# The post-norm of an output tile: gate first into on-chip memory, factor last in the operation that adds the stream

## The chip, the cores and the metric

The kernel runs on one core of one Trainium2 chip. The metric is the device time of one execution in microseconds (us). The core has a matrix engine (TensorE, PE in the profile; its weight loads are PEld), VectorE (DVE), ScalarE (ACT), GpSimd (POOL) and SyncE (SP), which issues the DMAs. Matrix products land in PSUM; everything else that is on the chip lies in SBUF.

## The reference

Four trunk layers work on 512 latent tokens and 256 context tokens of width 1024. Layer i uses the mixer i mod 3: latent attention with low-rank queries and keys (A, layers 0 and 3), banded window attention (B, layer 1), a gated long convolution by Fourier transforms (C, layer 2). Around every mixer stands the same frame. Cut to what matters here:

```python
def rmsnorm(x, g):
    return x * lax.rsqrt(jnp.mean(x * x, axis=-1, keepdims=True) + NORM_EPS) * g
...
h = rmsnorm(x, g_pre) * (1 + scale) + shift      # scale, shift, gate from the condition
y = mixer(h, ...)                                # ends in ... @ w_out
x = x + gate * rmsnorm(y, g_post)
```

Latent and context tokens have gates of their own. The last layer's output is the latent stream alone.

## The kernel before

The 768 tokens are six tiles of 128 (four latent, two context; the last layer handles four). A layer's mixer leaves its result, transposed, in one large block `og` of on-chip memory. Then `w_out_phase` goes over the tiles in a given order; below, tile 0 to 5 means the place in that order. For each tile it does the following.

- It splits the tile of `og` into a high and a low part (L613, L614) and multiplies both with the output weights: 48 matmuls of 128x512 (L622) into one of two PSUM tiles, `pb_70` and `pb_69`, which take turns. Each is 128x1024 in float32.
- `post` makes the new stream of the tile. ScalarE squares the product and sums along the row (L564); GpSimd makes the factor of the norm of the sum (`rstd`, L358 and L359: a scale and shift, and a power of minus one half); DVE multiplies the product by factor and gate, in place in PSUM (L566); DVE adds the stream to it (L567); SyncE stores the stream (L568).
- `pre` of the next layer follows at once, on the same tile: Square of the stream (L534), `rstd` on GpSimd, DVE's scaling into a slot `xs` (L537), eight transposes of 128x128 on PE (L543), scale and shift of the eight results back into `xs`, half of them on ScalarE (L548) and half on DVE (L550), and the split of `xs` into high and low part (L555 on ScalarE, L556 on DVE). After L556 `xs` is free.

Next the following layer's projections use the same two PSUM tiles: L577 to L579 where the channels stand on the partitions (keys and the like of layers 1 and 3), L588 behind layer 1. L442 are small matmuls that make the later layers' shifts, scales and gates. L230 (ScalarE) and L233 (GpSimd, in places DVE) split weights that a DMA has brought.

Slots of on-chip memory come from an arena of 13,760 float32 words per partition. `fs(D)` asks for one part of 1,024 words. While `og` is held, it takes 6,144 words, and seven parts are left for the streams of the tiles (`xt`), for `xs`, and for weights on their way. Of the first free ones, at most six (`turns_f`), the part freed longest ago is given out. Where the part has had another user, the new writer waits for the old reader.

The code is written tile by tile, but the order on each engine is not the order of the code: the framework's scheduler simulates the program on a timeline with its own costs and places every instruction on its engine. It also makes the semaphores. So an edit in `post` can move instructions of other lines.

Of the kernel before, what the change touches and what calls it, by code (L numbers as in the profile page):

```python
# [16 lines left out]
ALU = mybir.AluOpType  # L17
# [3 lines left out]
D = 1024  # L21
# [249 lines left out]
class Kern:  # L271
# [287 lines left out]
    def post(self, L, t, ys, xt, g):  # L559

        nc = self.nc
        s = 0 if t < 4 else 1
        ssq = self.col()
        nc.scalar.activation(self.trash, ys, AF.Square, accum_out=ssq)  # L564
        self.rstd(ssq, D)
        nc.vector.scalar_tensor_tensor(ys, ys, ssq, g[s].ap, op0=ALU.mult, op1=ALU.mult)  # L566
        nc.vector.tensor_tensor(xt.ap, xt.ap, ys, op=ALU.add)  # L567
        nc.sync.dma_start(out=self.xd[L + 1][t], in_=xt.ap)  # L568


# [1254 lines left out]
```

## Time and profile before

| quantity | value |
|---|---|
| time, median of three runs | 1950.36 us |
| the three runs | 1950.36, 1953.75 and 1942.91 us |
| the profiled execution's own time | 1947.24 us |
| its span in the profile | 1945.5 us |
| its mean granted TensorE clock | 0.989 of full speed |
| L566 / L567, mean of one | 1.29 / 1.22 us, 22 times each |
| L564, the Square | 1.00 us and 0.19 for its sum |

The span is what the profile shows between the first and the last instruction; the execution's own time contains a little around it. A row of the timeline gives the start, the duration, the engine, the line, the operation, what it writes and reads, and how many neighbours were put together; in brackets stands how long the engine was idle before it and what ended that. `pa` and `pb` are PSUM tiles, `arena_f`, `arena_r`, `swing_F` and `swing_R` parts of SBUF, `small` the column of sums and factors.

### The profile page before, as it was taken

How to read it: one execution, taken by the hardware profiler on the slowest of the kernel's cores; microseconds unless marked ns; L12 is line 12 of the kernel's file. 1: busy time of each engine (PE TensorE's matmuls, PEld its weight loads, DVE VectorE, ACT ScalarE, POOL GpSimd, SP SyncE). 2: the span in 40 equal slices, each digit the busy share in tenths (PEclk: the TensorE clock that was granted, in tenths of full speed). 3: DMA queues.
4: the chain of work that ended last, by engine and by line, in shares of the span. 5: the costliest groups of instructions: out<-in, count | busy, mean ns of one | idle time of the engine just before them, and what ended most of it. 6: DMA issues, size and time to landing. Idle time of an engine off the chain costs nothing. (4 is left out here: it accounts for less than half of the span.)

```text
span 1945.5 us, 30306 instructions
## 1 busy us (share of the span) xinstructions
PE 1815.3 (93%) x11628; PEld 1572.0 (81%) x11628; DVE 1176.2 (60%) x2364; ACT 812.6 (42%) x1687; POOL 517.7 (27%) x523
## 2 busy tenths in 40 slices
PE   5879799999999899999989999999998999999998
PEld 3657588999988888888868789999987777889986
DVE  6794234777755277777774356655567553477663
ACT  3473222545544255665654422222222353354451
POOL 5551000000213321222231444444445121000120
PEclk9999899999999999999999999999999999999999
DMA  7967420011133122222362622222222335310121
GB/s 218 270 185 232 140 75 25 23 33 34 55 108 109 55 65 66 77 77 66 119 204 100 200 82 77 75 74 71 75 65 68 115 121 153 86 34 23 44 76 54
DMA packets 186356, 186.31 MB, mean 96 GB/s; under 512 B 16600, under 2 KB 164952, under 8 KB 186212
## 3 DMA queue, kind: packets, MB, share of 16 engines
q1 hardware_dynamic: 186212, 184.39, 30.8%
q8 instruction: 91, 1.49, 0.3%
q14 instruction: 53, 0.43, 0.1%
HBM read 160.24 MB, written 24.12 MB: 95 GB/s over the span
## 5 line engine op out<-in xcount | busy, mean ns | idle before, releaser
L588 PE MATMUL pb<-arena_r 128*128 128x512 f32 (+1 forms) x1488 | 280.5, 342 | 2.1 <-DVE arena_f L1519 1.1
L341 ACT ACTIVATE arena_r<-pa 128x384 fp32r<-128x384 f32 (+2 forms) x382 | 175.2, 478 | 200.2 <-PE pa L898 67.2
L588 PEld LDWEIGHTS pb<-arena_r 128*128 128x128 f32 x1488 | 229.3, 189 | 33.1 <-ACT arena_r L1451 1.5
L342 DVE TENSOR_TENSOR arena_r<-pa,arena_r 128x384 fp32r<-128x384 f32 (+2 forms) x382 | 199.8, 537 | 79.4 <-ACT arena_r L341 77.4
L588 PE MATMUL pa<-arena_r,swing_R 128*128 128x512 f32 (+1 forms) x816 | 165.9, 355 | 0.6 <-DVE arena_r L342 0.4
L588 PEld LDWEIGHTS pa<-arena_r,swing_R 128*128 128x128 f32 x816 | 132.2, 188 | 21.8 <-DVE arena_r L342 0.6
L873 PE MATMUL pb<-arena_r 128*128 128x384 f32 (+1 forms) x720 | 141.4, 336 | 3.0 <-ACT arena_r L341 1.8
L233 POOL TENSOR_TENSOR swing_R<-arena_f,swing_R 128x1024 fp32r<-128x1024 f32 (+1 forms) x33 | 76.6, 2325 | 204.0 <-ACT swing_R L230 154.1
L873 PEld LDWEIGHTS pb<-arena_r 128*128 128x128 f32 x720 | 119.0, 188 | 5.1 <-ACT arena_r L341 2.5
L668 POOL TENSOR_TENSOR arena_f<-arena_f 128x128 f32<-128x128 f32 (+1 forms) x44 | 20.8, 474 | 364.0 <-DVE small L881 180.2
L622 PE MATMUL pb<-arena_r 128*128 128x512 f32 x480 | 115.2, 393 | 0.0
L358 POOL TENSOR_SCALAR small<-small 128x1 f32<-128x1 f32 x68 | 18.1, 266 | 350.8 <-ACT trash L704 136.0
L622 PEld LDWEIGHTS pb<-arena_r 128*128 128x128 f32 x480 | 89.5, 188 | 20.0 <-issue 1.1
L233 POOL TENSOR_TENSOR arena_r<-swing_F,arena_r 128x1024 fp32r<-128x1024 f32 x34 | 82.8, 2437 | 79.8 <-ACT arena_r L230 73.6
L912 PE MATMUL pa<-arena_r 128*128 128x256 f32 x624 | 91.4, 286 | 2.1 <-DVE arena_r L342 2.1
L912 PEld LDWEIGHTS pa<-arena_r 128*128 128x128 f32 x624 | 81.7, 189 | 4.8 <-ACT arena_r L341 2.5
L1068 PE MATMUL pa<-swing_R,arena_r 128*128 128x256 f32 x576 | 80.3, 289 | 5.1 <-DVE arena_f L348 3.8
L877 DVE TENSOR_REDUCE small<-pb 128x1 f32<-128x768 f32 (+1 forms) x80 | 67.5, 846 | 21.6 <-PE pb L873 20.8
L880 ACT ACTIVATE arena_f<-pb,small 128x768 f32<-128x768 f32 (+1 forms) x80 | 65.2, 816 | 33.6 <-DVE small L878 27.2
L1068 PEld LDWEIGHTS pa<-swing_R,arena_r 128*128 128x128 f32 x576 | 72.9, 192 | 7.3 <-DVE arena_f L348 5.2
L1049 PE MATMUL pa<-arena_r,swing_R 128*128 128x512 f32 (+1 forms) x384 | 74.2, 342 | 2.7 <-DVE arena_r L1075 1.1
L442 PE MATMUL pa<-arena_f,cst 128*32 128x256 f32 x744 | 55.7, 398 | 20.2 <-DMA arena_f<-in_w_mod_dram 20.1
(267 smaller groups left out, 4209.8 us busy)
## 6 DMA issues: line engine op xcount, KB each, us to landing
arena_f<-in_w_mod_dram SPq DMA_DIRECT2D x93, 512.0 KB, 4.8
swing_F<-in_c_w_in_dram SPq DMA_DIRECT2D x31, 512.0 KB, 4.9
kd<-arena_f SPq DMA_DIRECT2D x48, 256.0 KB, 3.7
arena_f<-in_a_w_in_dram SPq DMA_DIRECT2D x24, 512.0 KB, 3.7
arena_f<-kd SPq DMA_DIRECT2D x16, 768.0 KB, 5.2
arena_f<-in_b_w_in_dram SPq DMA_DIRECT2D x20, 512.0 KB, 3.7
x<-arena_f SPq DMA_DIRECT2D x18, 512.0 KB, 4.1
arena_f<-in_a_w_out_dram SPq DMA_DIRECT2D x16, 512.0 KB
```

The source lines that it names most:

```text
L233: eng.tensor_tensor(lo, view, hi.bitcast(F32), op=ALU.subtract)
L341: self.nc.scalar.activation(hi, src, AF.Copy)
L342: self.nc.vector.tensor_tensor(lo, src, hi.bitcast(F32), op=ALU.subtract)
L442: nc.tensor.matmul(ps[32 * j:32 * j + 32, n0:n0 + 256], self.cst[:, 4 * kh + j, :], w[:, j, :], start=(kh == 0), stop=(kh == 1), skip_grou ...
L588: nc.tensor.matmul(out, l, rhs(part, k, i), start=(k == 0 and q == 0), stop=(k == kt - 1 and q == 2))
L622: nc.tensor.matmul(ys[:, 512 * hf:512 * hf + 512], ov[:, part, k], wt[:, 0, 512 * hf:512 * hf + 512], start=(k == 0 and q == 0), stop=(k = ...
L873: nc.tensor.matmul(S[:, 512 * b:512 * b + w], l, r[:, k0 + w * b:k0 + w * b + w], start=(q == 0), stop=(q == 4))
L877: nc.vector.tensor_reduce(mx, Sv, axis=AX.XY, op=ALU.max)
L880: nc.scalar.activation(pr.v(nb, w), Sv, AF.Exp, bias=mx, scale=sc, accum_out=sm)
L912: nc.tensor.matmul(o[:, 0:256], vv[:, a_, kt % 3, P * hh:P * hh + P], ptv[i // nh][:, b_, i % nh], start=(i == 0 and q == 0), stop=(i == n ...
L1049: nc.tensor.matmul(o, l[:, k], self.h_at(h, part, k, t0, n), start=(k == 0 and i == 0), stop=(k == KD - 1 and i == 2))
L1068: nc.tensor.matmul(ps[:, 0:256], self.h_at(h, part, k, P * t, P), w, start=(k == 0 and i == 0), stop=(k == KD - 1 and i == 2))
```

## The change

`post` multiplies the product by the gate alone and puts the result into a slot `yg` of on-chip memory. This operation no longer reads the factor. The factor comes in the second operation, which multiplies `yg` by it and adds the stream, with both inputs in SBUF. The PSUM tile is read by the Square and by the first product, and written no more.

```diff
         s = 0 if t < 4 else 1
+        yg = self.fs(D)
         ssq = self.col()
         nc.scalar.activation(self.trash, ys, AF.Square, accum_out=ssq)
         self.rstd(ssq, D)
-        nc.vector.scalar_tensor_tensor(ys, ys, ssq, g[s].ap, op0=ALU.mult, op1=ALU.mult)
-        nc.vector.tensor_tensor(xt.ap, xt.ap, ys, op=ALU.add)
+        nc.vector.tensor_tensor(yg.ap, ys, g[s].ap, op=ALU.mult)
+        nc.vector.scalar_tensor_tensor(xt.ap, yg.ap, ssq, xt.ap, op0=ALU.mult, op1=ALU.add)
+        yg.free()
         nc.sync.dma_start(out=self.xd[L + 1][t], in_=xt.ap)
```

Two lines more stand above the rest, so every later line has a number that is two higher in the program after: the product is L567, the scale-and-add L568, the store L570, the Square L565, the matmul of the tile L624 (L622 before), the key projection L579 to L581 (L577 to L579), the projection behind layer 1 L590 (L588). `pre` keeps its numbers.

The scheduler places much anew. The following pieces show the engines at three transitions from one layer to the next.

First, DVE at the end of layer 0, from the post of tile 3 to the second operation of the post of tile 5. Before:

```order
L614 TENSOR_TENSOR arena_r<-arena_f,arena_r 128x1024
L566 SCALAR_TENSOR_TENSOR pb_69<-pb_69,small,arena_f 128x1024
L567 TENSOR_TENSOR arena_f<-arena_f,pb_69 128x1024
L550 TENSOR_SCALAR arena_f<-pa_65,ab 128x128 x4
L556 TENSOR_TENSOR arena_r<-arena_f,arena_r 128x8x128
L537 TENSOR_SCALAR arena_f<-arena_f,small 128x1024
L566 SCALAR_TENSOR_TENSOR pb_70<-pb_70,small,arena_f 128x1024
L550 TENSOR_SCALAR arena_f<-pa_67,ab 128x128 x4
L567 TENSOR_TENSOR arena_f<-arena_f,pb_70 128x1024
L556 TENSOR_TENSOR arena_r<-arena_f,arena_r 128x8x128
L537 TENSOR_SCALAR arena_f<-arena_f,small 128x1024
```

And after:

```order
L567 TENSOR_TENSOR arena_f<-pb_69,arena_f 128x1024
L568 SCALAR_TENSOR_TENSOR arena_f<-arena_f,small 128x1024
L537 TENSOR_SCALAR arena_f<-arena_f,small 128x1024
L550 TENSOR_SCALAR arena_f<-pa_67,ab 128x128 x4
L556 TENSOR_TENSOR arena_r<-arena_f,arena_r 128x8x128
L567 TENSOR_TENSOR arena_f<-pb_70,arena_f 128x1024
L568 SCALAR_TENSOR_TENSOR arena_f<-arena_f,small 128x1024
L537 TENSOR_SCALAR arena_f<-arena_f,small 128x1024
L567 TENSOR_TENSOR arena_f<-pb_69,arena_f 128x1024
```

Before, the post of a tile (L566, L567) stands ahead of the end of the pre of the tile before (L550, L556) or between its rows. After, in layers 0 and 1, the product of tile t+1 (t from 0 to 3) stands behind L556 of tile t: `yg` of tile t+1 has the part of the arena that `xs` of tile t had.

Second, PE in the same stretch; the rows with `pb_70` are tile 4, those with `pb_69` tile 5, L577 and L579 the first keys of layer 1. Before:

```order
L622 MATMUL pb_70<-swing_R,arena_r 128x512 x11
L543 MATMUL pa_68<-ident,arena_f 128x128 x4
L543 MATMUL pa_65<-ident,arena_f 128x128 x4
L622 MATMUL pb_70<-swing_R,arena_r 128x512 x7
L622 MATMUL pb_70<-arena_r 128x512 x30
L622 MATMUL pb_69<-swing_R,arena_r 128x512 x9
L543 MATMUL pa_66<-ident,arena_f 128x128 x4
L543 MATMUL pa_67<-ident,arena_f 128x128 x4
L622 MATMUL pb_69<-swing_R,arena_r 128x512 x9
L622 MATMUL pb_69<-arena_r 128x512 x30
L577 MATMUL pb_70<-swing_R,arena_r 128x256
```

And after:

```order
L624 MATMUL pb_70<-swing_R,arena_r 128x512 x18
L624 MATMUL pb_70<-arena_r 128x512 x14
L543 MATMUL pa_68<-ident,arena_f 128x128 x4
L543 MATMUL pa_65<-ident,arena_f 128x128 x4
L624 MATMUL pb_70<-arena_r 128x512 x16
L624 MATMUL pb_69<-swing_R,arena_r 128x512 x18
L624 MATMUL pb_69<-arena_r 128x512 x19
L543 MATMUL pa_66<-ident,arena_f 128x128 x4
L543 MATMUL pa_67<-ident,arena_f 128x128 x4
L624 MATMUL pb_69<-arena_r 128x512 x11
L579 MATMUL pb_70<-swing_R,arena_r 128x256
```

The transposes of tile 2 stood behind 11 matmuls of tile 4 and now stand behind 32; those of tile 3 stood behind 9 of tile 5 and now behind 37. Those of tile 4 stood behind 8 key matmuls and now behind 12, those of tile 5 behind some 96 and now behind 48. In layer 1 the transposes of tiles 1, 2 and 3 stood behind 11, 8 and 15 matmuls of tiles 3, 4 and 5 and now stand behind 34, 29 and 37; those of tile 4 stood behind 5 matmuls L588 and now behind 24.

Third, ScalarE at the end of layer 1, from the Square of tile 4 (`pb_70`) to the Square of tile 5 (`pb_69`). Before:

```order
L564 ACTIVATE trash,small<-pb_70 128x1024
L548 ACTIVATE arena_f<-pa_66,ab 128x128 x4
L534 ACTIVATE trash,small<-arena_f 128x1024
L555 ACTIVATE arena_r<-arena_f 128x8x128
L230 ACTIVATE arena_r<-swing_F 128x1024 x3
L564 ACTIVATE trash,small<-pb_69 128x1024
```

And after:

```order
L565 ACTIVATE trash,small<-pb_70 128x1024
L230 ACTIVATE arena_r<-swing_F 128x1024
L548 ACTIVATE arena_f<-pa_66,ab 128x128 x4
L230 ACTIVATE arena_r<-swing_F 128x1024
L555 ACTIVATE arena_r<-arena_f 128x8x128
L230 ACTIVATE arena_r<-swing_F 128x1024
L534 ACTIVATE trash,small<-arena_f 128x1024
L565 ACTIVATE trash,small<-pb_69 128x1024
```

The L230s, which split the first weights of layer 2, stood behind the L555 of tile 3 and now stand between its L548 and around it.

At the end of layer 2 DVE's rows are as follows after the change, with the engines and queues whose semaphores each waits for:

```order
L567 TENSOR_TENSOR arena_f<-pb_69,arena_f 128x1024 [waits Activation_49]
L556 TENSOR_TENSOR arena_r<-arena_f,arena_r 128x8x128 [waits Activation_49]
L568 SCALAR_TENSOR_TENSOR arena_f<-arena_f,small 128x1024 [waits DMAHW2_49,DMAHW3_49,DVE_49,Pool_49]
L537 TENSOR_SCALAR arena_f<-arena_f,small 128x1024 [waits DVE_49,Pool_49]
L567 TENSOR_TENSOR arena_f<-pb_70,arena_f 128x1024 [waits DMAHW1_49,DVE_49,Activation_49]
```

The product waits for ScalarE, that is for the Square of its tile, and not for PE, although it needs nothing that the Square makes. There it stands ahead of the L556 of the tile before, not behind it.

## The prediction

> **What bounds the kernel now.** I read the page first, then the waits of TensorE (PE), then the timeline around each of the four stages in which the changed lines run.
>
> ```profile
> span 1945.5 us, 30306 instructions
> PE 1815.3 (93%) x11628; PEld 1572.0 (81%) x11628; DVE 1176.2 (60%) x2364; ACT 812.6 (42%) x1687; POOL 517.7 (27%) x523
> ```
>
> PE is busy for 93% of the span, VectorE (DVE) for 60%. So an edit on DVE pays only where PE waits for it. The window of tile 3 of layer 0's output projection (its length, then the busy time of PE, of its weight loads, of DVE, ACT and POOL) shows PE without a gap:
>
> ```profile
> 574.90:587.00 12.10, 12.10 (x58) 9.99 (x57) 7.00 (x9) 5.56 (x10) 1.51 (x4) 1.00 0.33 111
> ```
>
> DVE is idle for 5 of the 12 us there. In the list of PE's waits (total, times, longest) the old lines of post appear twice, and a neighbour of them, the reading of the keys, once:
>
> ```profile
> PE pb L577 <- DVE arena_f L667: 3.5, 3, 1.4
> PE pb L577 <- DVE arena_f L567: 2.6, 1, 2.6
> PE pb L588 <- DVE arena_f L567: 1.0, 1, 1.0
> ```
>
> The first group lies behind layer 0, the second behind layer 2, the third behind layer 1. Behind layer 3 nothing runs on PE; there the chain of post itself is the end of the program:
>
> ```profile
> 1937.34 1.02 ACT L564 ACTIVATE trash<-pb 128x1024 bf16<-128x1024 f32 x1 [9.91 <-issue]
> 1938.26 0.19 ACT L564 ACTIVATION_READ_ACCUMULATOR trash<-pb 128x1 f32 x1
> 1938.81 0.55 POOL L359 TENSOR_TENSOR small<-small,mhalf 128x1 f32<-128x1 f32 x1
> 1939.39 1.29 DVE L566 SCALAR_TENSOR_TENSOR pb<-pb,small,arena_f 128x1024 f32<-128x1024 f32 x1 [8.48 <-POOL small L359]
> 1940.72 1.22 DVE L567 TENSOR_TENSOR arena_f<-arena_f,pb 128x1024 f32<-128x1024 f32 x1
> ```
>
> **Part 1, the operations.** Two DVE operations go and two come, 22 times each. These are the two that go, and the nearest one with both operands in SBUF:
>
> ```profile
> L566 DVE SCALAR_TENSOR_TENSOR pb<-pb,small,arena_f x22: 1281/1292/1293, 552.4 to 1939.4; 128x1024 f32<-128x1024 f32 x22
> L567 DVE TENSOR_TENSOR arena_f<-arena_f,pb x22: 1208/1216/1222, 554.2 to 1940.7; 128x1024 f32<-128x1024 f32 x22
> L556 DVE TENSOR_TENSOR arena_r<-arena_f,arena_r x23: 1206/1224/2589, 112.5 to 1603.5; 128x1024 fp32r<-128x1024 f32 x23
> ```
>
> The new product (PSUM and SBUF in, SBUF out) has the operands of the old L567, so 1.22 us, between 1.21 and 1.29. The new scale-and-add (scalar_tensor_tensor, both inputs in SBUF) is not in the trace. It lies between 1.21 (L556's fastest) and 2.59 (L556's slowest); I take 1.29, the old L566, the row with its operation. So DVE's work is unchanged: 2.51 us a tile before and after.
>
> The slow L556 has its reason beside it, and so has a small operation later:
>
> ```profile
> 604.95 2.59 DVE L556 TENSOR_TENSOR arena_r<-arena_f,arena_r 128x1024 fp32r<-128x1024 f32 x1 [0.22 <-ACT arena_r L555]
> 601.46 2.42 POOL L233 TENSOR_TENSOR swing_R<-arena_f,swing_R 128x1024 fp32r<-128x1024 f32 x1 [0.46 <-ACT swing_R L230]
> 604.04 2.41 POOL L233 TENSOR_TENSOR swing_R<-arena_f,swing_R 128x1024 fp32r<-128x1024 f32 x1 [0.17 <-ACT swing_R L230]
> 603.52 1.21 DVE L567 TENSOR_TENSOR arena_f<-arena_f,pb 128x1024 f32<-128x1024 f32 x1
> ```
>
> L556 began inside a GpSimd L233 and ended 1.1 us after it, as if it had stood still until 606.45. The old L567, with an operand in PSUM, took its usual 1.21 us though it began while the L233 before ran (601.46 to 603.88). Thus the new scale-and-add can lose up to 1.3 us where it meets an L233, which the old pair did not. The Trainium skill, page "SBUF — State Buffer", section "SBUF: two separate sides", says the same as a rule against this change: a DVE operation with two SBUF inputs and a GpSimd operation that reads SBUF share a port pair, and the later one waits for the whole of the other. By it two or three of the 22 would pay, +2 to +4 us in all; by the old pair's row, none. I take none into the sum and both into the range.
>
> **Part 2, the end.** Before, from the Square's start at 1937.34 to L567's end at 1941.94: Square, then GpSimd's factor until 1939.36, then 1.29, then 1.22. After: the order lists the product as waiting for ScalarE's Square, so it starts at about 1938.5, ends 1939.75 with the factor computed beside it, and the scale-and-add ends at 1941.05: **−0.9 us**. If the product ran beside the Square, as the change intends, it would end at 1938.6 and the factor (1939.36) would set the rest: 1940.65, −1.3.
>
> **Part 3, the coupling.** This decides the sum. The product needs a slot of on-chip memory, and the free parts of that arena are few while the mixer's output is held. In layers 0 and 1 the product of tile t+1 gets the part that tile t's scaled copy xs has just left; the order shows it, since the product stands behind the L556 of the tile before. So post of t+1 waits for pre of t, whose transposes (L543) the order has put far back among the matmuls of the next tiles. How long a round takes is read from this tile:
>
> ```profile
> 578.20 1.03 PE L543 MATMUL pa<-ident,arena_f 128*128 128x128 f32 x8
> 578.84 1.51 ACT L548 ACTIVATE arena_f<-pa,ab 128x128 f32<-128x128 f32 x4 [2.09 <-PE pa L543]
> 581.64 1.06 ACT L555 ACTIVATE arena_r<-arena_f 128x1024 fp32r<-128x1024 f32 x1
> 582.73 1.23 DVE L556 TENSOR_TENSOR arena_r<-arena_f,arena_r 128x1024 fp32r<-128x1024 f32 x1 [1.19 <-ACT arena_r L555]
> ```
>
> L543's start to L548's end is 2.15; L555 adds 1.1 and L556 1.25: 4.5 us until the part is free, and 1.3 more until the product has emptied the bank, **5.8**. From the stream's new value to the next L543 it takes the second Square, GpSimd's factor and L537:
>
> ```profile
> 591.81 1.06 ACT L534 ACTIVATE trash<-arena_f 128x1024 bf16<-128x1024 f32 x1 [0.19 <-DVE arena_f L567]
> 593.32 0.55 POOL L359 TENSOR_TENSOR small<-small,mhalf 128x1 f32<-128x1 f32 x1
> 595.52 0.75 DVE L537 TENSOR_SCALAR arena_f<-arena_f,small 128x1024 f32<-128x1024 f32 x1
> ```
>
> 591.71 (L567's end) to 593.87 and 0.75 more: 2.95 us.
>
> Layer 0, on before's clock, with tile 4 starting at 586.85:
>
> ```profile
> 586.85 2.73 PE L622 MATMUL pb<-swing_R,arena_r 128*128 128x512 f32 x11
> 603.79 6.99 PE L622 MATMUL pb<-arena_r 128*128 128x512 f32 x30
> 615.91 0.39 PE L577 MATMUL pb<-swing_R,arena_r 128*128 128x256 f32 x1 [1.44 <-DVE arena_f L667]
> 616.26 0.28 PE L579 MATMUL pb<-swing_R,arena_r 128*128 128x256 f32 x1
> 616.38 0.28 PE L577 MATMUL pb<-swing_R,arena_r 128*128 128x256 f32 x1
> ```
>
> A matmul takes 0.233 us (6.99 by 30), a tile of 48 and 8 transposes 11.9 (its transposes the rest), a key matmul 0.12 (from 616.26 to 616.38). Tile 2's transposes now stand behind 32 of tile 4's matmuls, at 594.25; tile 3's bank is free at 600.1, while PE wants it for tile 5 at 598.75: +1.4. Tile 5 then runs from 600.15, tile 3's transposes behind 37 of it at 608.7, tile 4's bank is free at 614.55; the keys want it at 612.05: +2.5. Tile 4's scale-and-add ends at 615.85, its L543 can start at 618.8, and PE, with 12 key matmuls, is there at 616.0: +2.8. In the same way the other bank comes 0.9 late and tile 5's transposes 1.9. Together 9.5. It takes the place of before's waits on L667, 3.5 in all: **+6.0** (range +3 to +9, since keys that start later may still wait).
>
> Layer 1, by the same steps, from these rows:
>
> ```profile
> 1053.63 2.03 PE L622 MATMUL pb<-swing_R,arena_r 128*128 128x512 f32 x8
> 1077.97 1.06 ACT L230 ACTIVATE arena_r<-swing_F 128x1024 fp32r<-128x1024 f32 x1 [0.79 <-PE pb L622]
> 1075.47 0.64 PE L442 MATMUL pa<-arena_f,cst 128*32 128x256 f32 x8
> 1077.26 7.11 POOL L233 TENSOR_TENSOR arena_r<-swing_F,arena_r 128x1024 fp32r<-128x1024 f32 x3 [4.17 <-ACT arena_r L230]
> 1087.18 0.64 PE L442 MATMUL pa<-swing_F,cst 128*32 128x256 f32 x8 [1.03 <-DMA swing_F<-in_w_mod_dram]
> 1088.87 7.30 PE L588 MATMUL pb<-arena_r 128*128 128x512 f32 x24 [1.05 <-DVE arena_f L567]
> ```
>
> Tile 1's transposes now stand behind 34 matmuls of tile 3 (1049.7), so the bank for tile 4 is free at 1055.55 against 1053.65: +1.9; tile 5 starts 0.9 later again. Then ScalarE has one L230 between the Square of tile 4 and tile 3's L548, and one between L548 and L555. The second waits for the last matmuls of tile 5, which free its place; with these at 1080.9 (two tiles of 11.9 and the L442 between, 0.6, from 1055.55, and the 0.9), L230 ends at 1081.8, L555 at 1082.9, L556 at 1084.1, the product at 1085.4, where the next projection wants the bank at 1080.9: +4.5. The waits of 1.03 and 1.05 vanish in that: **+5.2** (range +3 to +7).
>
> Layer 2 has room (layer 2 gives the product parts of its own but once), so the saving comes through:
>
> ```profile
> 1588.10 1.00 ACT L564 ACTIVATE trash<-pb 128x1024 bf16<-128x1024 f32 x1
> 1590.78 1.29 DVE L566 SCALAR_TENSOR_TENSOR pb<-pb,small,arena_f 128x1024 f32<-128x1024 f32 x1 [0.78 <-POOL small L359]
> 1594.38 0.42 PE L577 MATMUL pb<-swing_R,arena_r 128*128 128x320 f32 x1 [2.62 <-DVE arena_f L567]
> 1606.53 0.44 PE L710 MATMUL pa<-ident,arena_f 128*128 128x128 f32 x2 [1.99 <-DVE arena_f L707]
> ```
>
> The Square ends at 1589.2, so the product could empty the bank by 1590.5; PE came for it at 1591.76 and got it at 1594.38. The 2.62 goes. What is late next is L707 at 1606.53 behind two small chains on GpSimd; earlier keys bring perhaps half of its 1.99: **−3.6** (range −4.5 to −1).
>
> **Sum.** 6.0 + 5.2 − 3.6 − 0.9 = **+6.7 us** on the profiled 1947.24 us, so 1953.9. The median of the runs shown is 1950.36, 3.1 above that execution, so I forecast 1957. The insides of layers 1 to 3 are ordered anew too; nothing here prices that, and I allow 5 us either way.
>
> **The rivals.** (a) *The change does what it says.* The coupling costs nothing, because PE comes to the L543s earlier than my positions say or the banks are wanted later, and each transition gains: 2.6 + 1.0 + 1.4 + 0.9, so −6, 1944. For it speaks that before shows PE waiting for just these lines; against it, that the product stands behind L556 in the order. (b) *The coupling multiplies.* Each late bank makes the next tile's pre late; where GpSimd's L233 lies between (three in a row at 1077 behind layer 1, two at 601 to 606 in layer 0), factor and scale-and-add wait for up to 2.4 us, and everything behind is a bank later. One such hit on each of the two transitions (2 × 2.4), at the top of their ranges (9 + 7), with layer 2 at −1 and the end at −0.9: +19, 1969. It decides from the point where an L233 ends after the product. For it speaks the row of 2.59; against it, that most L233s lie elsewhere. (c) *The new order inside the layers* gains more than the transitions lose: 1942.
>
> **How the numbers follow.** Forecast 0.48; (a) 0.20; (b) 0.24; (c) 0.08. Half a per cent, 9.75 us, is about what a measurement of this kernel can tell from no change. The forecast lies 3 us below that limit, so of its 0.48 I count 0.10 as slower and 0.38 within; of (a) 0.07 faster and 0.13 within; of (b) 0.22 slower and 0.02 within; of (c) 0.05 faster and 0.03 within. Faster 0.12, within 0.56, slower 0.32. The range takes in (a) and (b) and cuts their far ends: 1942 to 1971.
>
> **What would show it.** Right: the product starts in layers 0 and 1 just behind an L556, many us after its Square; PE waits for the product at the starts of tile 5 and of the next projection, 1.5 to 4.5 us each, and for L537 at L543; behind layer 2 the wait of 2.6 is gone; the end is 0.9 shorter, with the product behind the Square. Wrong: products that start right after their Square everywhere; a wait of a different kind inside a mixer that is larger than these; a scale-and-add whose mean is far from 1.29.

## The result, and the profile after

| kernel | median | runs | ratio to before |
|---|---|---|---|
| before | 1948.26 us | 4, 1942.91 to 1953.75 | |
| after | 1982.32 us | 4, 1978.91 to 1988.54 | 1.017, 95% interval 1.0142 to 1.0198 |

The change makes the kernel 34 us slower. The forecast was 1957, with a range from 1942 to 1971. The profiled execution took 1978.91 us. Its page begins:

```profile
span 1977.1 us, 30282 instructions
PE 1829.5 (93%) x11628; PEld 1580.9 (80%) x11628; DVE 1196.0 (60%) x2364; ACT 810.3 (41%) x1687; POOL 526.7 (27%) x523
```

The same 11,628 matmuls: of the 31.6 us that the span grew, PE is idle for 17.4 more and busy for 14.2 more. It did no more work but did it at a lower clock, 0.982 for the whole span against 0.989. From 40 us to the last matmul the trace grants half the clock for 64.9 us after and for 37.5 us before; 27.4 us more at half the speed are, as an estimate, 13.7 of the 14.2. Not all of it is the change: 6.8 of the 27.4 us lie ahead of layer 0's output, where both kernels run the same, and other executions of the kernel before had clocks from 0.979 to 0.990. PE's waits (total, times, longest), those that touch the change:

```profile
PE pa L543 <- DVE arena_f L537: 8.3, 6, 1.9
PE pb L590 <- DVE arena_f L567: 7.5, 1, 7.5
PE pa L712 <- DVE arena_f L709: 5.8, 5, 2.8
PE pb L624 <- DVE arena_f L567: 4.8, 3, 2.3
PE pb L579 <- DVE arena_f L567: 2.7, 1, 2.7
PE pb L579 <- DVE arena_f L669: 2.6, 1, 2.6
PE pb L580 <- POOL swing_R L233: 2.3, 1, 2.3
```

Where before the old post held PE up for 3.6 us (2.6 and 1.0), the product L567 now holds it up for 15 (7.5, 4.8, 2.7), and the transposes wait 8.3 for L537 against 3.9.

To find where the time went, marks on PE were read from the timelines of all profiled executions: the first output matmul of layer 0 (533.5 before), the first matmul of layer 1's scores (681.7), the last of its values (1010.1), the first transposes of layer 2's transforms (1117.5), the last output matmul of layer 2 (1587.1) and the first transposes of layer 3's queries, L810 (1702.3). The table says by how much each stretch grew on before, in us, for the change and for the nine experiments below. The last column ends at the Square of the last tile, so the 0.9 us that the end of the program is shorter are not in the table. The first column is not the change: up to the first mark all kernels run the same, and executions differ there by up to 7 us. Each row is one execution, so that a stretch that runs as before can still differ by some 2 us (-1.9 behind layer 1 with new posts in layers 2 and 3 alone, -1.8 in layer 3 with a choice of three parts).

| kernel | to the first mark | layer 0's output and the way into layer 1 | inside layer 1 | layer 1's output and the way into layer 2 | layer 2 | into layer 3 | layer 3 |
|---|---|---|---|---|---|---|---|
| after | +1.9 | +9.9 | +11.9 | +14.4 | -4.8 | -0.6 | -0.2 |
| layer 0 alone | +4.1 | +9.9 | +12.2 | +2.0 | -0.9 | -1.7 | -0.2 |
| layer 1 alone | +3.1 | -1.1 | +0.4 | +9.1 | -0.3 | -1.7 | -0.3 |
| layers 2 and 3 | +2.0 | -0.1 | +0.6 | -1.9 | -0.7 | 0.0 | -1.1 |
| part freed last | +7.1 | +2.6 | +0.5 | +1.9 | -1.9 | -0.1 | -0.2 |
| slot alone | +2.6 | +0.5 | +10.8 | +5.7 | -1.7 | +1.7 | -0.2 |
| choice of three parts | +5.3 | +0.4 | -0.4 | -0.1 | +0.2 | -0.6 | -1.8 |
| tie alone | +0.6 | +7.1 | -0.3 | +9.3 | -3.4 | -0.1 | -0.2 |
| product in PSUM | +1.4 | -3.7 | +0.8 | -1.2 | +0.2 | -4.0 | -0.3 |
| one weight moved | +2.9 | -1.6 | +19.0 | +2.4 | +2.4 | +0.9 | -0.1 |

First, the way into layer 1. These rows of the timeline after (DVE and PE, numbers two higher than before) show the tie at work:

```profile
599.72 1.23 DVE L556 TENSOR_TENSOR arena_r<-arena_f,arena_r 128x1024 fp32r<-128x1024 f32 x1 [1.19 <-ACT arena_r L555]
600.98 1.22 DVE L567 TENSOR_TENSOR arena_f<-pb,arena_f 128x1024 f32<-128x1024 f32 x1
602.35 4.43 PE L624 MATMUL pb<-swing_R,arena_r 128*128 128x512 f32 x18 [1.58 <-DVE arena_f L567]
614.59 1.23 DVE L556 TENSOR_TENSOR arena_r<-arena_f,arena_r 128x1024 fp32r<-128x1024 f32 x1 [1.19 <-ACT arena_r L555]
615.85 1.22 DVE L567 TENSOR_TENSOR arena_f<-pb,arena_f 128x1024 f32<-128x1024 f32 x1
617.22 0.49 PE L579 MATMUL pb<-swing_R,arena_r 128*128 128x256 f32 x1 [2.71 <-DVE arena_f L567]
621.38 1.09 PE L543 MATMUL pa<-ident,arena_f 128*128 128x128 f32 x8 [1.32 <-DVE arena_f L537]
627.34 0.44 PE L580 MATMUL pb<-swing_R,arena_r 128*128 128x256 f32 x1 [2.25 <-POOL swing_R L233]
638.05 0.58 PE L579 MATMUL pb<-swing_R,arena_r 128*128 128x256 f32 x1 [2.60 <-DVE arena_f L669]
```

Each product starts right behind the L556 of the tile before, and PE starts right behind the product: 1.58 us late for tile 5, 2.71 for the keys. The next two rows are waits of PE that come after: 1.32 us for L537 at tile 4's transposes, and 2.25 us for the L233 that splits a weight of the keys. The last row is a wait of the kind that before had too (L669 was L667); the late keys did not absorb it.

The way into layer 2 shows the same, with two things that make it worse:

```profile
1111.95 1.06 ACT L230 ACTIVATE arena_r<-swing_F 128x1024 fp32r<-128x1024 f32 x1 [0.82 <-DMA swing_F<-in_c_w_in_dram]
1113.09 5.66 POOL L233 TENSOR_TENSOR arena_r<-swing_F,arena_r 128x1024 fp32r<-128x1024 f32 x2 [0.92 <-ACT arena_r L230]
1113.99 2.54 DVE L556 TENSOR_TENSOR arena_r<-arena_f,arena_r 128x1024 fp32r<-128x1024 f32 x1 [4.69 <-ACT arena_r L555]
1116.56 1.23 DVE L567 TENSOR_TENSOR arena_f<-pb,arena_f 128x1024 f32<-128x1024 f32 x1
1117.93 2.47 PE L590 MATMUL pb<-arena_r 128*128 128x512 f32 x5 [7.53 <-DVE arena_f L567]
```

The L230 that stands ahead of L555 waits for a weight's DMA, L556 then meets an L233 and takes 2.54 us instead of 1.23, and the first projection of layer 2 waits 7.53 us.

The end of the program went as forecast:

```profile
1969.81 1.02 ACT L565 ACTIVATE trash<-pb 128x1024 bf16<-128x1024 f32 x1 [9.90 <-issue]
1970.96 1.23 DVE L567 TENSOR_TENSOR arena_f<-pb,arena_f 128x1024 f32<-128x1024 f32 x1 [8.42 <-ACT trash L565]
1972.28 1.28 DVE L568 SCALAR_TENSOR_TENSOR arena_f<-arena_f,small 128x1024 f32<-128x1024 f32 x1
```

From the Square's start to the end of the last operation it is 3.75 us (1969.81 to 1973.56) against 4.60 (1937.34 to 1941.94). The product starts behind the Square, not beside it.

### The profile page after: what moved, and what is told of

Read it like the earlier page. It is cut to its first block, busy times and chain, and to the rows that moved or that the text cites. A ratio compares the mean times of both kernels' runs of the same rounds, so it can differ in the third digit from the quotient of the medians.

```text
span 1977.1 us, 30282 instructions
## 1 busy us (share of the span) xinstructions
PE 1829.5 (93%) x11628; PEld 1580.9 (80%) x11628; DVE 1196.0 (60%) x2364; ACT 810.3 (41%) x1687; POOL 526.7 (27%) x523
## 4 chain that ended last, share of the span: by engine, by line
PE 73%; DVE 12%; DMA 7%; ACT 4%; issue 3%; POOL 2%; SPq 0%; ACTq 0%; DVEq 0%; POOLq 0%
PE pb L590 11%; PE pb L624 11%; PE pa L590 10%; PE pb L875 5%; PE pa L914 4%; PE pa L1070 3%; PE pa L1051 3%; DMA arena_f<-in_w_mod_dram 3%; PE pa L1548 2%; PE pa L1581 2%; PE pb L579 2%; PE pb L580 2%; PE pb L581 2%; PE pa L900 2%; PE pa L1179 2%
## 5 line engine op out<-in xcount | busy, mean ns | idle before, releaser
L590 PE MATMUL pb<-arena_r 128*128 128x512 f32 (+1 forms) x1488 | 285.6, 345 | 7.5 <-DVE arena_f L567 7.5
L590 PEld LDWEIGHTS pb<-arena_r 128*128 128x128 f32 x1488 | 230.8, 191 | 39.8 <-issue 8.7
L590 PE MATMUL pa<-arena_r,swing_R 128*128 128x512 f32 (+1 forms) x816 | 166.0, 355 | 0.6 <-DVE arena_r L342 0.4
L590 PEld LDWEIGHTS pa<-arena_r,swing_R 128*128 128x128 f32 x816 | 132.2, 188 | 21.8 <-DVE arena_r L342 0.6
L233 POOL TENSOR_TENSOR swing_R<-arena_f,swing_R 128x1024 fp32r<-128x1024 f32 (+1 forms) x33 | 77.3, 2346 | 180.8 <-ACT swing_R L230 126.2
L624 PE MATMUL pb<-arena_r 128*128 128x512 f32 x480 | 117.2, 395 | 0.0
L233 POOL TENSOR_TENSOR arena_r<-swing_F,arena_r 128x1024 fp32r<-128x1024 f32 x34 | 86.8, 2555 | 74.3 <-ACT arena_r L230 74.3
L624 PEld LDWEIGHTS pb<-arena_r 128*128 128x128 f32 x480 | 88.9, 188 | 20.7 <-issue 2.4
L442 PE MATMUL pa<-arena_f,cst 128*32 128x256 f32 x744 | 57.8, 404 | 25.4 <-DMA arena_f<-in_w_mod_dram 25.3
L624 PE MATMUL pb<-swing_R,arena_r 128*128 128x512 f32 x288 | 74.5, 409 | 5.2 <-DVE arena_f L567 4.8
```

The costliest lines, as they stand in the source:

```text
L233: eng.tensor_tensor(lo, view, hi.bitcast(F32), op=ALU.subtract)
L442: nc.tensor.matmul(ps[32 * j:32 * j + 32, n0:n0 + 256], self.cst[:, 4 * kh + j, :], w[:, j, :], start=(kh == 0), stop=(kh == 1), skip_grou ...
L590: nc.tensor.matmul(out, l, rhs(part, k, i), start=(k == 0 and q == 0), stop=(k == kt - 1 and q == 2))
L624: nc.tensor.matmul(ys[:, 512 * hf:512 * hf + 512], ov[:, part, k], wt[:, 0, 512 * hf:512 * hf + 512], start=(k == 0 and q == 0), stop=(k = ...
```

## The experiments

Ratios are to runs of the kernel before on the same chip, and a difference in us is that of the two medians. Unless told, the edits are to the changed kernel.

**Layer by layer.** In the first three the new operations stand in some layers only, the old ones in the others, chosen by this edit (here for layer 0):

```diff
-        yg = self.fs(D)
+        yg = self.fs(D) if L == 0 else None
...
-        nc.vector.tensor_tensor(yg.ap, ys, g[s].ap, op=ALU.mult)
+        nc.vector.tensor_tensor(yg.ap, ys, g[s].ap, op=ALU.mult) if yg else nc.vector.scalar_tensor_tensor(ys, ys, ssq, g[s].ap, op0=ALU.mult, op1=ALU.mult)
...
```

Layer 0 alone:

> Only the posts of layer 0 are the new ones; layers 1 to 3 keep the old two operations. In the profile of the full change the time was lost in three stretches: about 10 us from layer 0's output tiles to layer 1's keys, about 16 inside layer 1's attention, about 14 from layer 1's output tiles into layer 2. Theory A (slot coupling, and an order of layer 1 that follows from layer 0's new posts): the first two come back here, +26 us on the kernel before, the third not. Theory B (the loss inside layer 1 belongs to layer 1's own posts or to weights loaded for them): only the first, +10 us.

Measured: 1972.37 us, ratio 1.0122 (1.0092 to 1.0152), +22 us. Both first stretches are there in full (+9.9 and +12.2), so the loss inside layer 1 comes from layer 0's post. Theory A holds, B falls.

Layer 1 alone:

> Only the posts of layer 1 are new. Theory A: layer 0's transition and the inside of layer 1 are as before, and the waits for the product and the lower clock behind them at the start of layer 2 are there: +10 to +14 us. Theory B: the inside of layer 1 loses its 16 us here, so +26 to +30.

Measured: 1956.19 us, ratio 1.0034 (1.0019 to 1.0049), +6 us. The wait is there: by the first transforms of layer 2 it has lost 8.4 us (11.5 less 3.1), and some 2 come back behind them. Nothing is lost inside layer 1. Theory A has the place right and the size at the start of layer 2; at the end less is left than it said.

Layers 2 and 3:

> Only the posts of layers 2 and 3 are new, where nearly every product has a part of the arena of its own. Theory A (no tie, so the saving comes through): the wait of 2.6 us at the first key tile of layer 3 is gone and the end is 0.9 shorter, -2 to -5 us in all. Rival (the full change gained nothing from layer 2 to layer 3, since what is late next takes the place of the wait): -1 us, the end alone.

Measured: 1947.91 us, ratio 0.9995 (0.9975 to 1.0016). No difference that can be measured; the time alone cannot tell theory A (-2 to -5 us) from the rival (-1). The trace speaks for the rival: the stretch into layer 3 is as long as before (0.0), the wait for the bank is gone, and in its place PE waits 1.5 us for L537 at the transposes and up to 2.5 for L709. In the full change the same waits stand at the same place (PE, layer 3's first keys):

```profile
1630.21 1.22 PE L543 MATMUL pa<-ident,arena_f 128*128 128x128 f32 x8 [1.88 <-DVE arena_f L537]
1639.80 0.44 PE L712 MATMUL pa<-ident,arena_f 128*128 128x128 f32 x2 [2.85 <-DVE arena_f L709]
```

1.88 and 2.85 us, where before had 2.62 and 1.99: the stream's pre and the keys' norm are late next.

**Another part for the product.** `yg` takes the part freed last, not the one freed longest ago:

```diff
-        free = free[:turns]
+        free = free if last else free[:turns]
...
-        _, _, si, o = min(free)
+        _, _, si, o = max(free) if last else min(free)
...
-        yg = self.fs(D)
+        yg = self._need(self.F, self.F.slot(D, 1024, 6, last=True), D)
```

> All posts new, but the product takes the part of the arena that was freed last (the stream of the tile before) instead of the one freed longest ago (its scaled copy xs). The transposes stand again where they stood before among the matmuls (at 161, 204 and 247 of layer 0's 288 against 158, 203 and 249 before, and 162, 224 and 277 in the changed kernel). Theory A (the tie to xs costs the transitions): the first transition loses at most 2 us on the kernel before, the third too, so the time falls by 20 or more from the changed kernel, to 1945 to 1962 depending on the order inside layer 1. Rival (the product is late because it waits for the Square, and the two operations on memory of the chip meet GpSimd): still 1975 to 1985.

Measured: 1955.80 us, ratio 1.0024 (1.0008 to 1.0041). Of the 34 us 5 are left, with another choice of part and the same operations. Theory A holds in the main; the rival, with 1975 to 1985, falls. This choice takes away two things at once: the tie to `xs`, and the loss inside layer 1 (+0.5), which the next experiments trace to where a weight lies. But the first stretch still loses 2.6 and gains nothing. One cause can be seen there, in the timeline of this kernel:

```profile
608.63 3.50 DVE L568 SCALAR_TENSOR_TENSOR arena_f<-arena_f,small 128x1024 f32<-128x1024 f32 x1
608.65 2.40 POOL L233 TENSOR_TENSOR swing_R<-arena_f,swing_R 128x1024 fp32r<-128x1024 f32 x1 [0.45 <-ACT swing_R L230]
```

The scale-and-add beside an L233 took 3.50 us instead of 1.28, more than the 2.59 that the prediction gave as its bound. What this costs the whole program was not tried by itself.

**The slot alone.** The old two operations, and a slot that nobody writes:

```diff
         yg = self.fs(D)
...
-        nc.vector.tensor_tensor(yg.ap, ys, g[s].ap, op=ALU.mult)
-        nc.vector.scalar_tensor_tensor(xt.ap, yg.ap, ssq, xt.ap, op0=ALU.mult, op1=ALU.add)
+        nc.vector.scalar_tensor_tensor(ys, ys, ssq, g[s].ap, op0=ALU.mult, op1=ALU.mult)
+        nc.vector.tensor_tensor(xt.ap, xt.ap, ys, op=ALU.add)
         yg.free()
```

> The kernel before, its two operations unchanged; post only asks the arena for a part of 1,024 words and gives it back without writing it. Nothing is computed otherwise, only who gets which part afterwards. PE's order inside layer 1 is then the changed kernel's, row for row, while the post of a tile again stands ahead of the end of the pre before it. Theory C (the loss inside layer 1 comes from where the parts lie: layer 1's weights go round in three parts instead of four, and the scheduler makes another order of it): +14 to +18 us, all of it inside layer 1. Rival (the loss comes from the new operations or from the late start of layer 1): within 3 us of before.

Measured: 1968.24 us, ratio 1.0089 (1.0069 to 1.0110), +18 us, with +0.5 behind layer 0 and +10.8 inside layer 1 (and 3 of the 5.7 up to layer 1's last output matmul). The rival falls: the loss inside layer 1 needs neither the new operations nor a late start. It was expected that all of the loss lies inside layer 1; 5.7 us of it came behind.

What the slot moved can be told from the arena. At the start of layer 1 one weight that was loaded ahead still holds its part. Five blocks for the probabilities and their sums (three of 656 words, two of 256) are then placed at the lowest free addresses, and the later weights go round in what is left (addresses in steps of 16 words):

```
                 weight held   the five blocks                weights go round in
before           540           384 to 538                     540, 604, 668, 732
slot, change     412           476 to 614, and 384 to 399     412, 668, 732
```

With the weight at 412 the blocks spill into a third part, and three are left for the weights instead of four.

**A choice of three parts.** The kernel before, with one number changed:

```diff
-        self.W.cap_w, self.W.cap_d, self.turns_f = 3, 1, 4
+        self.W.cap_w, self.W.cap_d, self.turns_f = 3, 1, 3
```

> The kernel before with one number changed: in layer 1 weights on their way may take only the first three free parts instead of four. PE's order inside layer 1 stays nearly that of before (748 of 755 rows). Theory C1 (a weight that has to wait for its part is what costs): +8 to +16 us. Theory C2 (the three parts matter only through the order that the scheduler makes of them): 0 to +3 us.

Measured: 1951.79 us, ratio 1.0009 (0.9994 to 1.0024), and -0.4 inside layer 1. The edit does less than theory C1 needs. The choice is among the first three parts that are free at the moment, and the blocks of layer 1 still go round in 540, 604, 668 and 732 (15 to 20 times in each). So no weight had to do with three parts. A narrower choice costs nothing that can be measured with nearly before's order on PE; whether a weight that waits for its part costs something (C1) was not tested.

**The tie alone.** The weights ahead of layer 1 are kept out of two parts, so that the five blocks fill two parts again, not three:

```diff
-                if (st[o:o + n] < self.BUSY).all():
+                if (st[o:o + n] < self.BUSY).all() and o not in self.avoid:
```

`avoid` is (412, 476) from layer 0's last output tile to the start of layer 1's mixer, and empty otherwise. (The expectation calls the five blocks rings for the rotations.) The blocks do not come to lie where before has them, as the expectation says: they lie at 0 to 154, the held weight at 284, and the later weights go round in 156, 220, 284 and 732. These are other addresses, but four parts for the weights as before.

> The changed kernel, but the weights that are loaded ahead at the end of layer 0 may not take the two parts in which layer 1 later puts its rings for the rotations, so these lie as before; PE's order inside layer 1 is that of before, row for row. The tie between the product and xs is kept in layers 0 and 1. Theory (the parts of the loss add up: tie about 10 us behind layer 0, about 6 behind layer 1 at the end of the program, and the rest inside layer 1): 1963 to 1969 on a before of 1950. Rival (the order inside layer 1 was only late because it started late): still 1978 or more.

Measured: 1961.98 us, ratio 1.0059 (1.0038 to 1.0079), +11.7 us, 1 us under the forecast. Inside layer 1 -0.3; behind layer 0 +7.1, from layer 1 into layer 2 +9.3, of which 3.4 come back in layer 2. The two losses are separate, and they add up: 11.7 here and 18 for the slot alone or 23 for the one weight moved (below) make 30 to 34, and the full change lost 34.

**One weight moved.** The kernel before with its old post and no slot; the weight that is held at the start of layer 1 is forced into the part at 412:

```diff
-        k = self.k
+        k = self.k; k.F.only = 412 if key == ('v', 1) else None
...
-                if (st[o:o + n] < self.BUSY).all():
+                if (st[o:o + n] < self.BUSY).all() and (self.only is None or o == self.only):
```

> The kernel before with its own post, without any slot in it; only one of the weights loaded ahead of layer 1 (the second half of the values' weight) is put into the part at 412 of the arena, as in the changed kernel, instead of the part at 540. The rings then spill into a third part, and the order of PE inside layer 1 is that of the changed kernel in 760 of 760 rows. Theory (the place of this one weight is the whole cause of the loss inside layer 1): +14 to +18 us, all between the start of layer 1's attention and its output tiles. Rival (the other parts that the slot shifted matter as well): under +8 us.

Measured: 1972.56 us, ratio 1.011 (1.0066 to 1.0154), +23 us, 19.0 of it inside layer 1. So the place of this one block is enough. It is somewhat more than was expected, and the interval is wide. PE's rows inside layer 1 stand in one and the same order in the four kernels that lose there: the change, layer 0 alone, slot alone and one weight moved (+10.8 to +19.0). They stand in before's order in layer 1 alone, layers 2 and 3, part freed last, tie alone and product in PSUM (-0.3 to +0.8). So the loss goes with the order; why this kernel lost 7 us more than the others with the same order was not found. PE's waits inside layer 1, first of before, then of this kernel:

```profile
PE pa L442 <- DMA arena_f<-in_w_mod_dram: 6.2, 10, 1.0
PE pa L1164 <- DVE arena_f L1150: 1.6, 2, 1.5
PE pa L1164 <- DVE arena_r L342: 1.4, 4, 0.7
```

```profile
PE pa L442 <- DMA arena_f<-in_w_mod_dram: 10.1, 10, 3.1
PE pa L1166 <- DVE arena_f L1152: 5.1, 5, 1.9
PE pa L1166 <- DVE arena_r L342: 3.8, 6, 1.7
```

Two kinds of wait grew most: of the small matmuls L442 for their weights, and of the probabilities' transposes for DVE; some others shrank. No single wait makes the loss. In the whole stretch PE was idle for 10.2 us more and busy for 8.8 more, at a clock of 0.97 against 0.99. In the new order the chains of the attention lie a little closer together: between the scores of a head and the transposes of its probabilities stand 73.5 matmuls in the median, against 79. That this makes the waits was not shown.

**The new operations without a slot.** The product stays in PSUM:

```diff
-        yg = self.fs(D)
...
-        nc.vector.tensor_tensor(yg.ap, ys, g[s].ap, op=ALU.mult)
-        nc.vector.scalar_tensor_tensor(xt.ap, yg.ap, ssq, xt.ap, op0=ALU.mult, op1=ALU.add)
-        yg.free()
+        nc.vector.tensor_tensor(ys, ys, g[s].ap, op=ALU.mult)
+        nc.vector.scalar_tensor_tensor(xt.ap, ys, ssq, xt.ap, op0=ALU.mult, op1=ALU.add)
```

> The new order of operations without a slot: the product of tile and gate is written in place in PSUM beside the factor, then one operation scales and adds the stream, reading PSUM. Theory (the idea is sound and only its slot costs): the bank and the stream come 0.9 us earlier per tile, the end is 0.9 shorter, layer 1 as before: -1 to -4 us. Rival (what is late next takes the place of everything but the end): 0 to -1 us.

Measured: 1940.56 us (8 runs) against 1950.29, ratio 0.9958 (0.9940 to 0.9975). It is the fastest kernel of the study, faster than both. It gains 3.7 us behind layer 0, 1.2 behind layer 1, 4.0 into layer 3 and the 0.9 at the end, more than was expected. The bank comes free one operation after the factor, not two, and no block of memory is needed for it. At layer 3's first keys PE now waits

```profile
1591.00 0.41 PE L579 MATMUL pb<-swing_R,arena_r 128*128 128x320 f32 x1 [1.20 <-DVE arena_f L568]
1601.90 0.44 PE L712 MATMUL pa<-ident,arena_f 128*128 128x128 f32 x2 [2.29 <-DVE arena_f L709]
```

## Why the prediction was wrong

**The step that failed** is the sentence in the sum that the insides of layers 1 to 3 "are ordered anew too; nothing here prices that, and I allow 5 us either way". Inside layer 1 the loss was 12 us, and some 3 to 4 more up to its last output matmul (layer 0 alone: 3.8, with layer 1's own post unchanged). It came from neither the operations nor the waits that the prediction followed: the slot shifted who gets which part, one weight landed at 412 instead of 540, five blocks spilled into a third part, and the scheduler made another order. The slot alone and the one moved weight show this, and the four kernels with that order are the four that lose inside layer 1. I had followed who gets the part of xs, and only in the tiles of the output projection.

**The tie** was foreseen, with its mechanism. Behind layer 0 the forecast had tile 5 late by 1.4 and the keys by 2.5; measured are 1.58 and 2.71. The stretch lost 9.9 against 6.0, just beyond its range to 9. Here the mechanism was right and its sizes were not. The late banks and transposes, put at 9.5 together, came to 5.6: beside the 1.58 and 2.71 only 1.32 for tile 4's transposes (put at 2.8), and nothing for the other bank and tile 5's transposes (put at 0.9 and 1.9). Of the 3.5 that I took off for before's waits on L667, 2.6 came back in one wait. Two things were in no term: the 2.25 us for an L233, and PE's 840 matmuls of this stretch, which kept it busy for 3.3 us longer at a clock of 0.97 against 0.99. Into layer 2 the wait was put at 4.5 and was 7.53: I had let the L230 wait for the last matmuls of tile 5, and it waited for a DMA, with L556 beside an L233 besides. In the tie alone 9 us were lost up to the first transforms and about 6 were left at the end of layer 2, against 5.2; the price of a lower clock behind the waits was in none of the terms.

**Behind layer 2** the forecast was -3.6, and nothing came of it: I saw that L707 was late next and still counted half of its 1.99 as a gain, while it became 2.85 and the transposes added 1.88. The rival in the third experiment, not my term, fits the traces.

**The end** (-0.9) measured -0.85, with the product behind the Square. **The operations**: the product takes 1.22 and the scale-and-add 1.28, as taken; two of the 22 reached 1.95 us, which lies within the bounds.

**The rivals.** Rival (a), -6 us if the change did what it says, is what the version in PSUM shows, with -10: the idea was sound, and the loss came with the slot. Rival (b), 1969, had the right side, but it looked for the loss at the transitions alone, and these, with their hits of L233, come to 1962 in the tie alone. What the hits cost by themselves was not tried. Rival (c) was the right place with the wrong sign. The chance of slower was 0.32.

What stays open: which rows of layer 1's new order cost most, and whether a weight's wait for one of three parts has a share in it. No run had before's order with three parts alone, and none the new order with four. Nor was it tried why 3 to 5 us come back in layer 2 behind a late start.

## What to carry to other kernels

A slot from a shared pool is part of a change's price, even if nothing is written to it: list who gets which part afterwards, over the whole program and not only around the edit, and compare the order of every stage before the time is forecast. Where a value can stay in the place that it has, try that first; here it turned a loss of 34 us into a gain of 10. When a wait is taken away at a place where another wait follows soon after (here 12 us later), count nothing for it until the next chain is followed to its end.

## What the runs showed of the hardware

A wait of PE can cost more than its length. Of the full change, two tiles' first matmuls, 18 each, behind waits of 1.58 and 2.31 us:

```profile
602.35 4.43 PE L624 MATMUL pb<-swing_R,arena_r 128*128 128x512 f32 x18 [1.58 <-DVE arena_f L567]
1083.68 5.99 PE L624 MATMUL pb<-swing_R,arena_r 128*128 128x512 f32 x18 [2.31 <-DVE arena_f L567]
```

0.25 us each behind the shorter wait and 0.33 behind the longer; behind the wait of 7.53 the first five took 0.49 each (2.47 by 5). The granted clock in the stretch from 614.5 to 701.7 us was 0.94, against 0.98 in the same work before. It changes between 1.00 and 0.50, in steps of 3.41 us: behind the wait of 2.71 it was 0.50 from 617.28 to 620.69 us. In the eleven traces, behind the first 40 us, all 109 steps at full clock in which PE was idle for more than 1.85 us were followed by a step at half the clock, and none was that had less than 1.50 us; between the two both happened. Short waits add up in this: one of the steps had 1.50 us of idle time and no wait above 0.62. The Trainium skill, page "TensorE: Matmul & The Clock Gate", section "Part 1: The HAM clock gate (the "warmup" mystery)", has PE fall to half its clock after an idle window of about 3.4 us and come back after as long a busy one; the halved speed agrees, but here idle time of about half of such a window was enough, and the measurement decides.

DVE operations with both inputs in SBUF that started beside a running GpSimd L233, or together with it, ended 1.1 us behind it, as if they had stood still until its end: L568 with 3.50 us above, L556 with 2.54 in the way into layer 2 (the first of the two L233s there ended at 1115.44). With an input in PSUM the same operation did not, in the version that keeps the product there:

```profile
L568 DVE SCALAR_TENSOR_TENSOR arena_f<-pb,small,arena_f x22: 1272/1282/1285, 555.5 to 1933.0; 128x1024 f32<-128x1024 f32 x22
1575.89 1.59 POOL L233 TENSOR_TENSOR arena_r<-arena_f,arena_r 128x640 fp32r<-128x640 f32 x1 [1.16 <-ACT arena_r L230]
1576.56 1.28 DVE L568 SCALAR_TENSOR_TENSOR arena_f<-pb,small,arena_f 128x1024 f32<-128x1024 f32 x1
```

1,285 ns is the longest of 22. Two of them met an L233; one of the two is the last row, which began inside an L233 and took 1.28 us. This agrees with the rule of the Trainium skill, page "SBUF — State Buffer", section "SBUF: two separate sides", that the prediction weighed.
